# Hybrid decoder trunk on one core: head sums taken token by token, SSD decays taken from banks that exist, and a conformer tail in token halves

## The chip, the cores and the metric

The kernel runs on 1 core of one Trainium2 chip. Times are device microseconds of one execution; a time is the median of several runs. Engines are named as the profile names them: PE (TensorE), PEld (its weight loads), DVE (VectorE), ACT (ScalarE), POOL (GpSimd) and SP (SyncE, which issues the transfers). The profiler took one execution; its page and its trace tell where that execution's time lies.

## The reference, cut to what matters

```python
D_MODEL, SEQ = 1024, 512
# layer 0: combined projection -> SSD heads and sliding-window attention -> output projection, residual
cb       = einsum("bclgn,bcsgn->bgcls", cc, bc)
y_diag   = einsum("bgecls,bcsgep->bclgep", cb[:, :, None] * decay_in, x)
y_off    = einsum("bclgn,bcgepn,bgecl->bclgep", cc, states, exp(a_cs))   # a_cs: running sum per head
y        = y_diag + y_off + xf * d_skip
y        = gated_group_rms_norm(y, z, w, groups)                        # two groups, y * silu(z)
q, k     = rms_norm(q, q_norm_w), rms_norm(k, k_norm_w)                  # per head of 64 channels
...      # windowed softmax with a sink per head and a T5 relative bias
# layer 1: conformer module
a, gate  = split(rms_norm(x) @ pw1 + pb1)
u        = a * sigmoid(gate)
v        = causal_depthwise_conv(u, dw, dwb)                             # 31 taps, 1024 channels
v        = silu(layer_norm(v, lnw, lnb))                                 # mean and variance over 1024 channels
x        = x + v @ pw2 + pb2
# behind each layer: gated MLP (D_FF = 2816) with a causal convolution of width 3, residual
```

## The kernel before, in words

512 tokens lie in the free dimension, 1024 channels in 8 tiles of 128 partitions. The program is the mixer (SSD and attention), a feed-forward block, the conformer, a second feed-forward block. Each large product takes float32 inputs split into a high and a low part, so each 128 x 128 block of weights costs three matmuls of 512 columns (L135 to L137); weights come three tiles ahead through `wr`, ACT casts the high part (L119) and DVE subtracts the low one (L120). A PSUM tile is called a bank: "mm" for products, "pa", "pb", "pc" for the rest.

In the mixer a scheduler orders the instructions of each engine; dependences, the number of buffers of a tag and the order of the code decide. A loop goes over x and q tiles: a projection, and beside it the SSD work of one head pair j. `ssd_states` spreads the row of each head over 128 partitions with a matmul (L483) for the mask exponentials. `ssd_outputs` multiplies masks and inputs (L515), spreads the pair's rows a second time with `pair_bcast` (L269), takes the exponential (L519) and multiplies it (L523) with the carried states' product (L522). `head_sums` squares a q or k tile (L535), casts and subtracts it into two parts (L537, L539) and adds, with two matmuls (L542), the sums over the two heads of 64 channels into rows of one bank `st_q`. After the last tile those rows are copied by ACT (L585) and transposed to token-wise columns (L588), and the inverse square roots of all heads are taken at once (from L593). Behind the attention `gr`, the inverse square root of the gated norm's moments, is spread over partitions (L163) before the output projection can go on.

The conformer is written out by hand: every engine runs its instructions as the code stands, within `manual_schedule`. Weight tiles are loaded in the order of use by SP. `project(2j)` gives the value, `project(2j+1)` the gate of tile j. `gate(j)` scales the gate (L863), takes the sigmoid (L865), forms `u` (L867), writes it to memory (L871) and reads it back in four shifted copies (L873) into `u4`, a tag of three buffers. `conv_pe(j)` convolves four taps at a time from these copies (L884, 24 groups of 4; 32 groups for tile 7) and subtracts a shift (L890); `add` and `sums` fold the result into running sums. `conv_pe(7)` runs in token halves. `tail_sums` (L941), `moments`, `spread` (L958), `normalise`, `residue` and `outputs` (L983 to L985) finish each half.

Of the kernel before, what the change touches and what calls it, by code (L numbers as in the profile page):

```python
# [7 lines left out]
F32 = mybir.dt.float32  # L8
F32R = mybir.dt.float32r
# [49 lines left out]
def kernel(ctx: ExitStack, tc: tile.TileContext, x, w_in, w_dt, w_out,  # L59
# [164 lines left out]
    def mixer(norm, nxt):  # L224
# [26 lines left out]
        sels = [mk([P, P], f"sel{i}", F32R) for i in range(2)]  # L251
        turn = [0]

# [4 lines left out]
        def pair_bcast(tag, j, r0):  # L258
            sel = sels[turn[0] % 2]
            if j == 8:  # L260
                for t in sels:
                    clear(t[64:P])
            turn[0] += 1
            a, b = (j, j + 8) if j < 8 else (16, 17)
            rr = slice(r0, r0 + 64)
            for half, q in zip(HALF, (a, b)):
                V.tensor_copy(sel[rr, half], con("pairs")[rr, q : q + 1].to_broadcast([64, 64]))
# [155 lines left out]
        for t in sels:  # L423
            clear(t[0:64])
        halves = mk([P, 265], "halves", F32R)
        V.tensor_copy(halves, con("halves"))
# [43 lines left out]
        def ssd_states(j):  # L470
# [21 lines left out]
            ssd[j] = [xdt, ms, xdd]  # L492
# [16 lines left out]
        def ssd_outputs(j):  # L509
            g = j // 4  # L510
            xdt, ms, sm = ssd.pop(j)
# [101 lines left out]
        bank = pair_bcast("pa", 8, 0)  # L613
# [14 lines left out]
        def attn_prep(j):  # L628
            bt = phase[0].tile([P, 2, 256], F32, name=nm("bt"), tag="bt", bufs=2)
            nc.sync.dma_start(bt, btab[j])  # L630
            bank = pair_bcast("pa", j, 0)
# [174 lines left out]
    def conformer(norm, nxt):  # L806
# [25 lines left out]
        def load(i):  # L832
            raws[i] = sbt("wr", 3, RING)
            nc.sync.dma_start(raws[i], pw1[(i % 2) * 8 + i // 2] if i < 16 else pw2[i - 16])
# [26 lines left out]
        def gate(j, va, pg):  # L861
            vg = sbt("cv", 2)
            V.tensor_tensor(vg, pg, norm.rb, op=ALU.mult)  # L863
            sg = sbt("th", 1)
            S.activation(sg, vg, AF.Sigmoid, bias=prm("pb1", 8 + j))  # L865
            u = ubuf[j % 3]
# [8 lines left out]
        def conv_pe(j, q=None, part=None):  # L875
            n, t0 = (T, 0) if q is None else (H, H * q)
            npe = GROUPS_PE[j]
            if part in (None, 0):
                cvp[j, q] = bank_of("pa")
            cv = cvp[j, q]  # L880
            gs = range(npe) if part is None else range(npe // 2 * part, npe // 2 * (part + 1))
            for g in gs:
# [323 lines left out]
```

## Time and profile before

| | |
|---|---|
| median of 3 runs | 1295.35 us |
| range of the runs | 1294.02 to 1297.88 us |
| profiled execution | 1297.84 us, its span 1296.0 us |
| mean granted TensorE clock | 0.996 |
| busy share of the span | PE 99%, DVE 66%, ACT 40%, POOL 10% |
| norm sums that open the first feed-forward block, the conformer, the second feed-forward block | at 381.7, 742.6 and 936.9 us |

The page gives busy time per engine and the chain that ended last. A busy PE includes matmuls that run at half clock, and the end of a matmul is modelled, so gaps on PE are read from the starts in the timeline and from the releaser in brackets. The windows view gives the granted clock of a stretch.

### The profile page before, as it was taken

Reading aid. Unit: us, or ns where it says so; the run is one execution under the profiler, and the core shown is the slowest. Engines: PE = TensorE matmul, PEld = TensorE weight load, DVE = VectorE, ACT = ScalarE, POOL = GpSimd, SP = SyncE. Lnnn points to the kernel's source line nnn. Section 1 sums busy time; section 2 is a strip of 40 time slices with the busy share of each in tenths; the row PEclk is TensorE's granted clock in tenths of the full one; section 3 lists DMA queues with packets and bytes.
Section 4 is the critical chain, followed back from the end, with each engine's and each line's share of the span. In section 5 each row is a group of like instructions: output and inputs, shape, how many; then the busy total and the mean of one; then the engine's idle time right before and its main releaser. Section 6 shows DMA issues by size and latency. Waiting matters only on the chain.

```text
span 1296.0 us, 16832 instructions
## 1 busy us (share of the span) xinstructions
PE 1281.3 (99%) x6443; PEld 1032.4 (80%) x6443; DVE 854.4 (66%) x1444; ACT 515.2 (40%) x812; POOL 124.2 (10%) x198
## 2 busy tenths in 40 slices
PE   9999999999999999999999999999999999999998
PEld 7878877778888888888888876658888888888887
DVE  7986769985348777777332377857677777774221
ACT  6465547863234333333232222226433333332120
POOL 0031204640210000000011100000600000000000
PEclk9999999999999999999999999999999999999999
DMA  6312222212333333323333265550333333333331
GB/s 225 98 50 65 66 65 66 66 44 71 98 101 96 96 95 96 96 94 94 102 90 103 90 181 146 154 151 2 117 98 98 98 98 98 96 92 102 108 118 39
DMA packets 40113, 125.13 MB, mean 97 GB/s; under 512 B 4704, under 2 KB 5088, under 8 KB 40032
## 3 DMA queue, kind: packets, MB, share of 16 engines
q1 hardware_dynamic: 39312, 123.50, 31.2%
q8 instruction: 51, 0.84, 0.3%
q10 hardware_dynamic: 720, 0.55, 0.2%
q14 instruction: 30, 0.25, 0.1%
HBM read 119.73 MB, written 4.29 MB: 96 GB/s over the span
## 4 chain that ended last, share of the span: by engine, by line
PE 78%; DVE 2%; POOL 0%; DMA 0%; issue 0%; ACT 0%; SPq 0%; ACTq 0%; POOLq 0%
PE mm L135 23%; PE mm L137 23%; PE mm L136 23%; PE pa L884 3%; PE pc L690 1%; PE pa L136 1%; PE pa L137 1%; PE pa L135 1%; PE pb L681 1%; DMA u<-du 0%; PE pb L163 0%; PE mm L984 0%; PE mm L985 0%; PE mm L983 0%; POOL lt L665 0%
## 5 line engine op out<-in xcount | busy, mean ns | idle before, releaser
L135 PE MATMUL mm<-xr,wh 128*128 128x512 f32 x1120 | 439.1, 392 | 0.0
L137 PE MATMUL mm<-xr,wl 128*128 128x512 f32 x1120 | 437.2, 390 | 0.5 <-DVE wl L362 0.5
L136 PE MATMUL mm<-xr,wh 128*128 128x512 f32 x1120 | 437.2, 390 | 0.0
L119 ACT CAST wh<-wr 128x1024 fp32r<-128x1024 f32 (+1 forms) x178 | 184.0, 1034 | 453.6 <-PE mm L136 411.3
L120 DVE TENSOR_TENSOR wl<-wr,wh 128x1024 fp32r<-128x1024 f32 (+1 forms) x178 | 214.5, 1205 | 156.2 <-ACT wh L119 151.0
L137 PEld LDWEIGHTS mm<-xr,wl 128*128 128x128 f32 x1120 | 210.3, 188 | 44.6 <-DVE wl L362 1.0
L135 PEld LDWEIGHTS mm<-xr,wh 128*128 128x128 f32 x1120 | 210.4, 188 | 43.6 <-issue 1.4
L136 PEld LDWEIGHTS mm<-xr,wh 128*128 128x128 f32 x1120 | 210.4, 188 | 43.0 <-DVE xr L183 0.4
L221 DVE TENSOR_TENSOR cv<-mm,nrb 128x512 f32<-128x512 f32 x116 | 79.6, 689 | 94.4 <-PE mm L137 90.4
L136 PE MATMUL mm<-g,wh 128*128 128x512 f32 x360 | 140.0, 389 | 0.0
L135 PE MATMUL mm<-g,wh 128*128 128x512 f32 x352 | 136.9, 389 | 0.0
L137 PE MATMUL mm<-g,wl 128*128 128x512 f32 x352 | 136.9, 389 | 0.0
L216 DVE SCALAR_TENSOR_TENSOR ct<-cv,par_ffn,ct 128x510 f32<-128x510 f32 (+1 forms) x176 | 131.1, 748 | 3.5 <-issue 0.4
L136 PEld LDWEIGHTS mm<-g,wh 128*128 128x128 f32 x360 | 67.6, 188 | 14.1
L135 PEld LDWEIGHTS mm<-g,wh 128*128 128x128 f32 x352 | 66.1, 188 | 13.7
L137 PEld LDWEIGHTS mm<-g,wl 128*128 128x128 f32 x352 | 66.1, 188 | 13.6
L193 POOL TENSOR_TENSOR nsum<-nsum,nsq 128x512 f32<-128x512 f32 x21 | 34.3, 1631 | 427.0 <-ACT nsq L192 427.0
L213 ACT ACTIVATE ct<-cv,par_ffn 128x512 f32<-128x512 f32 x88 | 71.4, 814 | 3.2 <-DVE cv L221 3.0
L789 ACT ACTIVATE th<-ct 128x512 f32<-128x512 f32 x44 | 27.8, 632 | 84.5 <-DVE ct L216 84.5
L800 DVE TENSOR_TENSOR h<-h,mm 128x512 f32<-128x512 f32 x16 | 11.0, 687 | 56.3 <-PE mm L137 56.3
L884 PE MATMUL pa<-u,dg 128*32 128x512 f32 (+1 forms) x464 | 45.0, 535 | 1.4 <-DMA u<-du 1.4
L884 PEld LDWEIGHTS pa<-u,dg 128*32 128x32 f32 x464 | 14.5, 110 | 27.0 <-issue 21.5
(308 smaller groups left out, 1393.4 us busy)
## 6 DMA issues: line engine op xcount, KB each, us to landing
wr<-w_up SPq DMA_DIRECT2D x88, 512.0 KB, 3.5
wr<-w_in SPq DMA_DIRECT2D x29, 512.0 KB, 3.5
wr<-w_dn SPq DMA_DIRECT2D x32, 448.0 KB, 3.3
wr<-pw SPq DMA_DIRECT2D x24, 512.0 KB, 6.0
wr<-w_out SPq DMA_DIRECT2D x16, 512.0 KB, 3.6
wr<-w_dn SPq DMA_DIRECT2D x16, 512.0 KB, 3.5
u<-du SPq DMA_DIRECT2D x28, 266.0 KB, 5.0
h<-x SPq DMA_DIRECT2D x8, 256.0 KB, 5.6
```

The source lines that it names most:

```text
L119: S.copy(wh[:, :n], raw[:, :n])
L120: V.tensor_tensor(wl[:, :n], raw[:, :n], f32(wh[:, :n]), op=ALU.subtract)
L135: TE.matmul(bank, wh[:, c], xh, start=first and i == 0, stop=False)
L136: TE.matmul(bank, wh[:, c], xl, start=False, stop=False)
L137: end = TE.matmul(bank, wl[:, c], xh, start=False, stop=last and i == n - 1)
L193: eng.tensor_tensor(self.sum, self.sum, sq, op=ALU.add)
L213: S.activation(t, v, AF.Identity, bias=bias, scale=w(taps - 1))
L216: V.scalar_tensor_tensor(t[:, s:], v[:, : T - s], w(k), t[:, s:], op0=ALU.mult, op1=ALU.add)
L221: V.tensor_tensor(v, bank, rb, op=ALU.mult)
L681: TE.transpose(tb[:, blk(b * 2 + e)], lt[:, e, blk(b)], ident)
L789: S.activation(sg, c, AF.Silu)
L884: TE.matmul(cv[quad(c), :n], diag[j][:, g, c, :], u4[j][:, c, 4 * g + t0 : 4 * g + t0 + n], start=g == 0, stop=g == npe - 1 and j < 2)
```

## The change

Three places change.

**SSD decays.** `ssd_states` takes, from the two banks it has anyway, an exponential of half the partitions each into `ec`, kept in the tag "att" until `ssd_outputs`. The second spread with `pair_bcast`, its two DVE casts and its exponential go. `pair_bcast` now serves the q and k scaling alone.

**Head sums.** The square, unsplit, is the stationary operand: four matmuls, each 128 tokens by 2 columns, write the sums token by token into `st_q`. The cast, the subtraction, the two matmuls of 512 columns, the copy and the four transposes go.

**Conformer.** The gate is projected first and its sigmoid taken before the value's projection ends; the loads swap accordingly. `gate(7)` is issued before the last part of `taps(6)`. The convolution of tile 4 moves out of the loop behind the sixteenth projection. Tiles 5 and 6 are convolved in token halves, interleaved with tile 7, whose first half now comes before the second halves of 5 and 6. The shifted copies of tile 7 are read in two parts (284 and 256 of 540 columns). The first output step comes before the second half's sums; the second evacuation on ACT stands behind the second `normalise`.

```diff
-        def pair_bcast(tag, j, r0):
+        def pair_bcast(tag, j):
...
@@ ssd_states
             ms = []
+            ec = sbt("att", 16)
             for e in range(2):
                 hd = e * 8 + j
                 bank = bank_of("pa")
                 TE.matmul(bank, pairs[:, hd : hd + 1].to_broadcast([P, P]), rows_t, start=True, stop=True)
+                S.activation(ec[HALF[e], P:], bank[HALF[e], P:], AF.Exp)
...
@@ ssd_outputs
-            cb2 = pair_bcast("pa", j, 64)
-            ec = sbt("d", 3)
-            S.activation(ec[:, P:], cb2[:, P:], AF.Exp)
...
@@ head_sums
-            hi = sbt("cv", 2, T, F32R)
-            V.tensor_copy(hi, sq)
-            lo = sbt("th", 1, T, F32R)
-            V.tensor_tensor(lo, sq, f32(hi), op=ALU.subtract)
-            w = halves[:, 137:265] if n == 8 else halves[:, 9 - n : 137 - n]
-            for i, o in enumerate((hi, lo)):
-                TE.matmul(st_q, w, o, start=n == 8 and i == 0, stop=n == 7 and i == 1)
+            for c in range(NB):
+                cols = slice(c * 18 + n, c * 18 + n + 9, 8) if n < 8 else slice(c * 18 + 16, c * 18 + 18)
+                TE.matmul(st_q[:, cols], sq[:, blk(c)], halves[:, 9:18:8], start=True, stop=True)
...
-        ssum = sbt("d", 3)[0:32]
-        S.copy(ssum, st_q[0:32])
-        bank = bank_of("pb")
-        for c in range(NB):
-            TE.transpose(bank[:, c * 32 : (c + 1) * 32], ssum[:, blk(c)], ident[0:32, 0:32])
-        stv = bank[:, : NB * 32].rearrange("p (c k) -> p c k", c=NB)[:, :, 0:18]
+        stv = st_q[:, : NB * 18].rearrange("p (c k) -> p c k", c=NB)
...
@@ conformer: gate
-            for s in range(4):
-                nc.sync.dma_start(u4[j][quad(s), :, 0:n], du.rearrange("(c p) n -> p c n", c=4)[:, :, s : s + n])
+            first = H + 4 * (GROUPS_PE[j] - 1)
+            for a, b in ((0, first), (first, n)) if j == 7 else ((0, n),):
+                for s in range(4):
+                    nc.sync.dma_start(u4[j][quad(s), :, a:b],
+                                      du.rearrange("(c p) n -> p c n", c=4)[:, :, s + a : s + b])
...
@@ conformer: order
-                if j >= 2:
+                if 2 <= j < 6:
                     conv_pe(j - 2)
...
-            conv_pe(5)
-            add(5)
-            sums(5)
-            conv_pe(6)
-            add(6)
-            sums(6)
-            conv_pe(7, 0, 0)
-            conv_pe(7, 0, 1)
+            gate(7, pa, sg)
+            taps(6, 1)
+            conv_pe(4)
+            add(4)
+            sums(4)
+            conv_pe(5, 0)
+            conv_pe(6, 0)
+            conv_pe(7, 0)
             evacuate(0)
-            conv_pe(7, 1, 0)
+            conv_pe(5, 1)
             bank = tail_sums(0)
             lr = moments(bank)
-            conv_pe(7, 1, 1)
-            evacuate(1)
+            conv_pe(6, 1)
             sa = spread(lr)
-            bank = tail_sums(1)
+            conv_pe(7, 1)
...
```

What stood on PE in one iteration of the mixer's loop before (`cv` and `th` are the two parts of the square, `b` the masks, `rows_t` the rows of decays, `bc` the states; the rows run from the head sums to the next pair's spread):

```order
L542 MATMUL mm_515<-cv_1084,halves 128x512
L515 MATMUL pb_1090<-b_985,c_973 64x128
...
L515 MATMUL pb_1090<-b_995,c_973 64x128
L542 MATMUL mm_515<-th_1086,halves 128x512
L515 MATMUL pb_1090<-b_985,c_973 64x128
...
L269 MATMUL pa_1101<-rows_t,sel_86 128x512
L522 MATMUL pc_1105<-bc_440,d_1043 128x128 x3
L474 MATMUL pb_1112<-ctile,xs_997 128x128 x4
```

And what stands there now, with the lines of the changed program (L531 is the head sums, L511 the mask products, L515 the states' product):

```order
L531 MATMUL mm_513<-ctile,nsq_1072 128x2 x4
L511 MATMUL pb_1078<-b_974,c_960 64x128
L511 MATMUL pb_1078<-b_985,c_960 64x128
...
L515 MATMUL pc_1087<-bc_438,d_1033 128x128 x3
L468 MATMUL pb_1094<-ctile,xs_987 128x128 x4
```

Three matmuls of 512 columns became four of 2 columns, and the eight mask products are no longer parted in two. Nine tiles have such sums; eight pairs had such a spread.

DVE at the gated norm before, from the last gate product to the last operation on `gr` (`nvar` is the moment, `rsi`, `rsh`, `rsq` steps of the inverse square root):

```order
L120 TENSOR_TENSOR wl_3356<-wr_3353,wh_3355 128x1024
L718 SCALAR_TENSOR_TENSOR ct_3174<-th_3172,cv_3170 128x512
L733 TENSOR_SCALAR nvar_3185<-pb_3180 128x4
L719 TENSOR_TENSOR xs_1429<-xs_1429,ct_3174 128x512
L142 TENSOR_SCALAR rsi_3188<-nvar_3185 128x4
...
L736 TENSOR_SCALAR gr_3187<-gr_3187 128x4
```

And in the changed program:

```order
L717 TENSOR_SCALAR nvar_3130<-pb_3125 128x4
L120 TENSOR_TENSOR wl_3301<-wr_3298,wh_3300 128x1024
L702 SCALAR_TENSOR_TENSOR ct_3119<-th_3117,cv_3115 128x512
L142 TENSOR_SCALAR rsi_3133<-nvar_3130 128x4
L146 TENSOR_SCALAR rsh_3136<-nvar_3130 128x4
L703 TENSOR_TENSOR xs_1404<-xs_1404,ct_3119 128x512
...
L720 TENSOR_SCALAR gr_3132<-gr_3132 128x4
```

The moment now stands ahead of the weight subtraction and of the last gate product. On PE 33 matmuls of the gate's projection stand between the attention's last product and the sums, where 12 stood, and 23 of the output projection between the sums and the spread of `gr`, where 25 stood.

PE in the conformer's tail before (`u` are the shifted copies, `dg` the taps on a diagonal, `krows,neg` the shift):

```order
L884 MATMUL pa_7335<-u_1408_7125,dg_7046 32x512 x24
L890 MATMUL pa_7335<-krows,neg 128x512
L884 MATMUL pa_7372<-u_1425_7242,dg_7163 32x512 x24
L890 MATMUL pa_7372<-krows,neg 128x512
L884 MATMUL pa_7409<-u_1440_7328,dg_7274 32x256 x32
L890 MATMUL pa_7409<-krows,neg 128x256
L884 MATMUL pa_7447<-u_1440_7328,dg_7274 32x256 x16
...
L884 MATMUL pa_7447<-u_1440_7328,dg_7274 32x256 x16
L890 MATMUL pa_7447<-krows,neg 128x256
L958 MATMUL pb_7520<-ctile,lr_7478 128x128 x4
```

And now (L873 is the convolution, L879 the shift, L932 the sums, L949 the spread):

```order
L873 MATMUL pa_7253<-u_1363_6953,dg_6864 32x512 x24
...
L873 MATMUL pa_7290<-u_1380_7070,dg_6991 32x256 x24
...
L873 MATMUL pa_7327<-u_1395_7156,dg_7108 32x256 x24
...
L873 MATMUL mm_7358<-u_1410_7239,dg_7188 32x256 x32
...
L873 MATMUL pa_7290<-u_1380_7070,dg_6991 32x256 x24
...
L932 MATMUL pb_7428<-ones,s_1259_6357 128x1
...
L873 MATMUL pa_7327<-u_1395_7156,dg_7108 32x256 x24
...
L949 MATMUL pb_7493<-ctile,lr_7442 128x128 x4
L873 MATMUL mm_7358<-u_1410_7239,dg_7188 32x256 x32
```

The whole convolution of tile 4 and half of those of tiles 5 and 6 now stand ahead of the first half of tile 7; behind the first half's sums stand a half of tile 6, the spread and the second half of tile 7.

## Rows read from the trace of the kernel before

**Rows 1.** The page's parts 1 and 4: busy time of each engine with its share of the span, and the chain of work that ended last, by engine.

```profile
PE 1281.3 (99%) x6443; PEld 1032.4 (80%) x6443; DVE 854.4 (66%) x1444; ACT 515.2 (40%) x812; POOL 124.2 (10%) x198
...
PE 78%; DVE 2%; POOL 0%; DMA 0%; issue 0%; ACT 0%; SPq 0%; ACTq 0%; POOLq 0%
```

**Rows 2.** The windows view, four stretches of the span. Columns: stretch, its length; busy time of PE, PEld, DVE, ACT and POOL (instructions); granted TensorE clock; DMA share; GB/s.

```profile
88.00:176.00 88.00, 88.00 (x488) 71.17 (x487) 59.75 (x112) 45.61 (x95) 19.00 (x24) 1.00 0.23 72
200.00:276.00 76.00, 73.42 (x561) 56.85 (x561) 68.61 (x232) 60.21 (x176) 44.91 (x123) 1.00 0.18 57
...
288.80:295.40 6.60, 6.60 (x23) 5.73 (x23) 5.42 (x11) 3.06 (x5) 0.00 (x0) 0.50 0.26 79
...
882.80:886.00 3.20, 3.15 (x13) 2.98 (x14) 2.89 (x14) 2.07 (x4) 0.00 (x0) 0.50 0.00 0
```

**Rows 3.** The timeline of PE in the loop over x and q tiles, in one iteration (91.32 to 94.61) and in the last one (169.56, 170.58). Columns: start, duration, engine, line, operation, count [idle before <- releaser].

```profile
91.32 0.39 PE L542 MATMUL mm<-cv,halves 128*128 128x512 f32 x1
...
92.23 0.50 PE L542 MATMUL mm<-th,halves 128*128 128x512 f32 x1
...
93.24 0.51 PE L269 MATMUL pa<-rows_t,sel 128*128 128x512 f32 x1
93.58 0.83 PE L522 MATMUL pc<-bc,d 128*128 128x128 f32 x6
94.25 0.60 PE L474 MATMUL pb<-ctile,xs 128*128 128x128 f32 x4
...
169.56 1.09 PE L515 MATMUL pb<-b,c 128*64 128x128 f32 x16
170.58 0.50 PE L269 MATMUL pa<-rows_t,sel 128*128 128x512 f32 x1
```

**Rows 4.** The timeline of PE at another place of the kernel that takes sums over the 128 channels of a tile with a matmul of one column (`tok_sum`, four matmuls, eight records), between two projections of the feed-forward block.

```profile
381.68 0.95 PE L157 MATMUL pb<-ones,nsum 128*128 128x1 f32 x8
382.49 0.48 PE L135 MATMUL mm<-xr,wh 128*128 128x512 f32 x1
382.81 0.40 PE L136 MATMUL mm<-xr,wh 128*128 128x512 f32 x1
383.04 0.39 PE L137 MATMUL mm<-xr,wl 128*128 128x512 f32 x1
```

**Rows 5.** The lines view of ACT between 60 and 300 us, shapes apart: count | busy, mean ns of one | idle before.

```profile
L519 ACT ACTIVATE d<-pa 128x384 f32<-128x384 f32 x8 | 3.9, 491 | 2.1 <-PE pa L269 2.1
```

**Rows 6.** The timeline of all engines at the end of the head sums, from the square of the last q tile to the transposes.

```profile
178.59 0.63 ACT L535 ACTIVATE nsq<-att 128x512 f32<-128x512 f32 x1
...
179.79 0.69 DVE L539 TENSOR_TENSOR th<-nsq,cv 128x512 fp32r<-128x512 f32 x1
...
180.54 0.19 PEld L542 LDWEIGHTS mm<-th,halves 128*128 128x128 f32 x1 [0.26 <-DVE th L539]
...
181.88 0.32 PEld L588 LDWEIGHTS pb<-ctile,d 32*128 32x128 f32 x4 [0.35 <-ACT d L585]
```

**Rows 7.** The timeline of DVE at the gated norm of the mixer: one step of the inverse square root, and the last operation on `gr`.

```profile
285.70 1.20 DVE L149 TENSOR_TENSOR rsq<-rsy 128x4 f32<-128x4 f32 x1
...
287.91 0.17 DVE L736 TENSOR_SCALAR gr<-gr 128x4 f32<-128x4 f32 x1
```

**Rows 8.** The timeline of PE at the same place: the last matmul ahead of the broadcast of `gr`, the broadcast itself, and the output projection behind it.

```profile
285.81 0.39 PE L135 MATMUL mm<-att,wh 128*128 128x512 f32 x1
288.23 1.53 PE L163 MATMUL pb<-ctile,gr 128*128 128x128 f32 x8 [2.03 <-DVE gr L736]
289.56 1.71 PE L157 MATMUL pb<-ones,bc 128*128 128x1 f32 x8
291.12 0.77 PE L136 MATMUL mm<-att,wh 128*128 128x512 f32 x1
...
295.54 0.44 PE L137 MATMUL mm<-att,wl 128*128 128x512 f32 x1
```

**Rows 9.** The timeline of PE in the tail of the conformer, from the end of the sixteenth projection (runs of equal matmuls in one row).

```profile
856.16 5.36 PE L884 MATMUL pa<-u,dg 128*32 128x512 f32 x48
...
861.88 5.36 PE L884 MATMUL pa<-u,dg 128*32 128x512 f32 x48
...
869.07 3.66 PE L884 MATMUL pa<-u,dg 128*32 128x256 f32 x64 [1.40 <-DMA u<-du]
...
872.98 1.93 PE L884 MATMUL pa<-u,dg 128*32 128x256 f32 x32
874.84 0.38 PE L941 MATMUL pb<-ones,s 128*128 128x1 f32 x2
...
876.72 1.93 PE L884 MATMUL pa<-u,dg 128*32 128x256 f32 x32
...
879.60 1.16 PE L958 MATMUL pb<-ctile,lr 128*128 128x128 f32 x8 [0.63 <-DVE lr L152]
...
882.85 0.58 PE L983 MATMUL mm<-dg,wh 128*128 128x256 f32 x1 [0.41 <-ACT dg L973]
...
888.37 0.39 PE L984 MATMUL mm<-g,wh 128*128 128x256 f32 x1 [0.70 <-DVE g L976]
```

**Rows 10.** The timeline of DVE and SP in the same stretch: the gated `u` of tile 7, and the issue of its four shifted copies.

```profile
858.19 0.75 DVE L867 SCALAR_TENSOR_TENSOR u<-cv,par_conf,th 128x512 f32<-128x512 f32 x1 [0.85 <-ACT th L865]
...
861.57 1.75 SPq L873 DMA_DIRECT2D u<-du  x4
```

More of the change, by code (lines that the diff above doesn't have):

```diff
@@ L256, in clear @@
             V.tensor_copy(t, f32(t))
-        def pair_bcast(tag, j, r0):
+        sels = [mk([P, P], f"sel{i}", F32R) for i in range(2)]
+        turn = [0]
+        def pair_bcast(tag, j):
             sel = sels[turn[0] % 2]
-            if j == 8:
-                for t in sels:
-                    clear(t[64:P])
             turn[0] += 1
[L264 to L267, printed above, removed]
+            for half, q in zip(HALF, (j, j + 8) if j < 8 else (16, 17)):
+                V.tensor_copy(sel[0:64, half], con("pairs")[0:64, q : q + 1].to_broadcast([64, 64]))
             bank = bank_of(tag)
@@ L859, in make_diag, with sigmoid, gate @@
             diag[j] = t
-        def gate(j, va, pg):
-            vg = sbt("cv", 2)
-            V.tensor_tensor(vg, pg, norm.rb, op=ALU.mult)
+        def sigmoid(j, pg):
+            vg = scaled(pg, norm.rb)
             sg = sbt("th", 1)
             S.activation(sg, vg, AF.Sigmoid, bias=prm("pb1", 8 + j))
+            return sg
+        def gate(j, pa, sg):
+            va = scaled(pa, norm.rb)
             u = ubuf[j % 3]
@@ L888, in conv_pe @@
                 TE.matmul(cvp["shift"], neg, krows, start=True, stop=True)
-            if j > 1 and part in (None, 1):
-                TE.matmul(cv[:, :n], neg, krows[:, t0 : t0 + n], start=False, stop=True)
+            if j > 1:
+                TE.matmul(cv, neg, krows[:, t0 : t0 + n], start=False, stop=True)
         def taps(j, part):
@@ L901, in taps, with add, sums @@
                     V.scalar_tensor_tensor(y[j], win(j, k), w(j, k), y[j], op0=ALU.mult, op1=ALU.add)
-        def add(j):
-            V.tensor_tensor(y[j], cvp.pop((j, None)), y[j], op=ALU.add)
-        def sums(j):
+        def add(j, q=None):
+            t = slice(0, T) if q is None else half(q)
+            V.tensor_tensor(y[j][:, t], cvp[j][:, t], y[j][:, t], op=ALU.add)
+        def sums(j, q=None):
+            t = slice(0, T) if q is None else half(q)
             if j == 0:
@@ L1000, in conformer @@
                 if j > 0:
-                    va = scaled(pa, norm.rb)
-                if j >= 2:
+                    sg = sigmoid(j, pg)
+                if 2 <= j < 6:
                     conv_pe(j - 2)
@@ L1005, in conformer @@
                     shift_mean()
-                pg = project(2 * j + 1)
+                pa = project(2 * j + 1)
                 if j == 0:
                     norm.spread()
-                    va = scaled(pa, norm.rb)
+                    sg = sigmoid(j, pg)
                 split_w(2 * j + 3)
@@ L1020, in conformer @@
                         sums(q)
-                if j >= 4:
+                if 4 <= j < 6:
                     sums(j - 2)
-                gate(j, va, pg)
-            pa = project(14)
+                gate(j, pa, sg)
+            pg = project(14)
             make_diag(7)
             split_w(16)
+            sg = sigmoid(7, pg)
             taps(6, 0)
-            va = scaled(pa, norm.rb)
-            pg = project(15)
+            pa = project(15)
             split_w(17)
+            gate(7, pa, sg)
@@ L1051, in conformer @@
+            add(6, 1)
+            sums(6, 1)
             sa = spread(lr)
-            bank = tail_sums(1)
-            obank = [bank_of(t) for t in ("mm", "mm", "mm", "pc")]
-            normalise(0, 0, sa)
-            for j in range(1, 8):
+            conv_pe(7, 1)
+            obank = [bank_of(t) for t in ("mm", "mm", "pc", "mm")]
+            for j in range(5):
+                normalise(j, 0, sa)
+                if j:
+                    residue(j - 1, 0)
+                if j == 1:
+                    evacuate(1)
@@ L1056, in conformer @@
+            outputs(0, 0)
+            lr = moments(tail_sums(1))
+            for j in range(5, 8):
                 normalise(j, 0, sa)
                 residue(j - 1, 0)
-                if j == 2:
-                    lr = moments(bank)
             residue(7, 0)
-            for j in range(8):
+            for j in range(1, 8):
                 outputs(j, 0)
-                if j == 4:
+                if j == 5:
                     sa = spread(lr)
```

57 lines of the change are left out of this document (29 added, 28 removed).

## The prediction, made before the changed kernel had run

> **What bounds the kernel now.** I read the page's busy times and chain first, then the windows of the stages that change, then PE's timeline in them. PE is busy 99% of the span and the chain of waits lies on PE for 78% [rows 1]: what the change takes out of PE's queue shows in the time, what it takes from other engines does not. The windows add that PE is not one thing everywhere. In the loop over x and q tiles PE is busy 88.00 of 88 us, DVE 59.75 and ACT 45.61; in the attention PE is busy 73.42 and DVE 68.61 of 76, so DVE sets part of the pace there; and two short stretches, 6.60 and 3.20 us, ran at the 0.50 granted clock, the lower of the two levels (1.2 for 2.4 GHz) [rows 2]. The two gaps worth having are at those two stretches: 2.03 us ahead of the spread of `gr` [rows 8] and some waits in the conformer's tail [rows 9].
>
> **Head sums and second spread, on PE.** In one iteration the stretch from the first 512-column sum (91.32) to the next pair's transposes (94.25) takes 2.93 us [rows 3]. What is left of it: sixteen mask products without a break, 169.56 to 170.58, 1.02; the states' product, 93.58 to 94.25, 0.67 [rows 3]. What comes in: four matmuls of two columns. The nearest row is the sum of one column over 128 channels, 128 weights each, eight records, 381.68 to 382.49, 0.81 [rows 4]. So 1.02 + 0.67 + 0.81 = 2.50, a gain of 0.43 each. Five iterations have both edits: -2.15. Two further spreads stand without sums: 93.24 to 93.58, 0.34 each [rows 3], -0.68. The last iteration has sums and spread with 0.23 + 0.33 + 0.34 against 0.81: -0.1. Three sums stand alone amid projections, where the old pair costs about 0.47 (two at the 0.23 spacing seen at 382.81 to 383.04) and the new 0.81 plus 0.09 by which the second matmul behind it is late (382.49 to 382.81 against 0.23) [rows 4]: +0.43 each, +1.3, a little less where the old pair stood apart. The four transposes go: about -0.4 [rows 6]. Sum -2.1. The bounds are what eight small records can cost: nothing beyond their issue would add another -6 (nine groups by 0.7); 1.2 each would eat it (+3.5). I keep the row.
>
> A page of the Trainium skill has a rule here: "TensorE: Matmul & The Clock Gate", section "Back-to-back issue gap", puts matmuls of 1 to 64 columns at an issue floor of about 25 ns. By it eight records would cost 0.2 us instead of 0.8, an estimate from that figure, and nine groups would give 5.4 us more. The row disagrees: 0.10 us for each record, each with 128 columns of weights to load.
>
> **The chain behind the head sums.** The last square ends at 179.22; the casts, the subtraction, the second matmul at 180.54, ACT's copy and the transposes at 181.88 follow [rows 6]. All but the sums go, so k and q scaling can begin some 1.4 us sooner. PE has projections to do meanwhile, so this moves work but does not add to the sum.
>
> **The exponentials.** ACT gives up eight of 491 ns [rows 5] and takes sixteen of the same width over half the partitions. I price them alike: +3.9 us over eight pairs, 0.5 each. ACT is busy 45.61 of 88 us there [rows 2], which hides them. They hold a "pa" bank 0.5 us longer ahead of the mask exponentials; if that cover is gone, the price is 8 x 0.5 = 4 at most.
>
> **The gated norm.** PE stands 2.03 us for `gr` [rows 8]. In the changed order the moment's first operation stands ahead of a weight subtraction and of the last gate product on DVE, and PE has two matmuls less (0.5 us) between sums and spread. Counted in DVE operations, `gr` then comes about as PE does, with 0.2 us to spare. Yet one step of four columns on DVE took 1.20 us where the last operation on `gr` took 0.17 [rows 7], a hold-up on DVE that may stay. I take 1.4 of the 2.03 as gained; ends 0 and 2.03.
>
> **The slow clock behind it.** After that gap PE ran 6.6 us at 0.50, until a matmul at 295.54 [rows 2, 8]; at full clock the same work takes half, 3.3. The wait of 1.40 at 869.07 was followed by no such row in the windows I read [rows 9], so a wait cut to about 0.6 should not bring the clock down. -3.3, and 0 as the other end.
>
> **The conformer's tail.** PE's work from the end of the sixteenth projection (856.16) is the same list as before plus the convolution of tile 4, which only changes place (5.72, as 856.16 to 861.88 [rows 9]). Splitting tiles 5 and 6 adds two more shifts of 256 columns and four more starts, about +0.8. What can go: waits of 1.40 (shifted copies), 0.63 (`lr`), 0.41 (`normalise`) and 0.70 (`residue`) [rows 9], together 3.14, and the 3.20 us at 0.50 [rows 2] which cost 1.5. Each is covered now: between first sums and their spread stands a half convolution of tile 6 (half of 5.72) against a chain of 2.9 (876.72 to 879.60 [rows 9]); between spread and outputs stands the second half of tile 7, 3.9 (869.07 to 872.98 [rows 9]); the first output step and the sums of the second half, 1.9 (874.84 to 876.72), give `normalise` time. -3.14 - 1.5 + 0.8 = -3.8.
>
> Against it stand the copies of tile 7. `u4` has three buffers, so they now wait for tile 4's convolution, which ends 5.3 us after 856.16 [rows 9]: 861.5. Before, they were issued at 861.57, after a round through memory that follows `u`, done at 858.94 [rows 10]; the sigmoid's early place saves nothing there, since the wait has taken its place. From issue to use it took 7.5 us before (861.57 to 869.07 [rows 9, 10]). PE reaches tile 7 now after 5.72 and two halves of about 3.07, 868.0. If the first part lands in the share of its bytes (284 of 540: 3.9 us) nothing waits; if each part costs as the whole, 1.1 us are lost; interleaved with the weights, up to 2.7. I take 0.3. Tail: -3.5.
>
> [...]
>
> **Sum.** -2.1 - 1.4 - 3.3 - 3.5 = -10.3. The profiled execution took 1297.84, which is 2.5 above the median, so I apply the difference to the median: 1295.35 - 10.3 = 1285.05.
>
> **The rivals.**
> (a) The stall at `gr` stays or moves, and the clock falls as before. Its support is the DVE step of 1.20 us [rows 7]. Left are -2.1 and -3.5: 1289.7.
> (b) The mixer's saving is lost in the attention, where DVE is busy 68.61 of 76 us [rows 2]: PE arrives sooner and waits longer, the stall stays, and the copies come 1 to 2 us late. Only some -2 to -3 is left: 1292.8. For it: DVE's share. Against: PE has projections to put between.
> (c) Slower. Each group of eight small records is 0.8 us in which PE moves few columns, and if the granted clock fell behind each of nine groups as it did behind `gr`, each would cost 3.3 [rows 2]: +30, less the 10 gained, about 1315. It decides from about four such falls. Against it: behind the group at 381.68 matmuls run at 0.23 spacing at once [rows 4].
> (d) The edits do their work, but PE's queue is short of ready projections throughout, and nothing changes: 1295.
>
> **How the numbers follow.** Forecast 0.48, (a) 0.32, (b) 0.12, (c) 0.05, (d) 0.03. 0.3% of 1295.35 is 3.9 us, about what a measurement of this kernel can tell from no change. Faster than 1291.5: the forecast, (a) and nearly half of (b), 0.85. Within: 0.10. Slower: 0.05. The forecast's own ends: -12.4 with the whole stall and a tail of -5, and another 2.5 if the attention's own gaps of 2.58 us [rows 2] shrink: 1280.5. Upward the range takes in (a) and the better half of (b): 1291.5. Left out is less than 0.2.
>
> **What would show it.** One iteration of the mixer at 2.5 us from the sums to the next transposes; eight records of the head sums at 0.8 us; no wait over 1 us ahead of the spread of `gr` and no 0.50 behind it; tile 7's first half starting behind tile 6's without a gap; the first output step without a wait, at clock 1.00. The prediction fails if the small matmuls bring the clock down, if a bank held for the new exponentials stops PE in the loop, or if the copies come late.

## The result, and the profile after

The changed kernel takes 1288.77 us (median of 5 runs, 1288.48 to 1288.92); before, on the same chip, took 1295.35 (5 runs, 1293.77 to 1297.88). The ratio is 0.9943, with a 95% interval of 0.9932 to 0.9955: faster by 6.6 us, where 10.3 were forecast. Its profiled execution took 1288.92, with a span of 1287.1 and a mean clock of 1.000; that of before had 1297.84, 1296.0 and 0.996, so the two profiles differ by 8.9.

The page's parts 1 and 4 of the changed kernel answer [rows 1]:

```profile
PE 1274.5 (99%) x6583; PEld 1035.6 (80%) x6583; DVE 839.2 (65%) x1411; ACT 518.8 (40%) x821; POOL 124.0 (10%) x198
...
PE 78%; DVE 2%; POOL 1%; DMA 1%; issue 0%; ACT 0%; SPq 0%; DVEq 0%; ACTq 0%; POOLq 0%
```

PE is busy 6.8 us less with 140 records more; the share of the chain is as before. So the page tells that time went from PE, not where. One iteration of the loop in PE's timeline answers [rows 3]:

```profile
90.32 0.95 PE L531 MATMUL mm<-ctile,nsq 128*128 128x2 f32 x8
91.20 1.09 PE L511 MATMUL pb<-b,c 128*64 128x128 f32 x16
92.22 0.94 PE L515 MATMUL pc<-bc,d 128*128 128x128 f32 x6
93.00 0.60 PE L468 MATMUL pb<-ctile,xs 128*128 128x128 f32 x4
```

From the sums to the transposes 93.00 - 90.32 = 2.68 us instead of 2.93; 2.50 was forecast. Eight small records take 0.88 here, where 0.81 was priced, and the states' product 0.78 for 0.67.

PE's timeline at the gated norm answers [rows 8], with the windows view of the stretch behind it (columns as in [rows 2]):

```profile
285.03 0.39 PE L136 MATMUL mm<-att,wh 128*128 128x512 f32 x1
286.20 1.13 PE L163 MATMUL pb<-ctile,gr 128*128 128x128 f32 x8 [0.78 <-DVE gr L720]
287.17 0.95 PE L157 MATMUL pb<-ones,bc 128*128 128x1 f32 x8
287.98 0.48 PE L137 MATMUL mm<-att,wl 128*128 128x512 f32 x1
288.29 0.39 PE L135 MATMUL mm<-att,wh 128*128 128x512 f32 x1
```

```profile
284.00:290.00 6.00, 5.22 (x32) 4.33 (x31) 3.49 (x9) 1.63 (x2) 1.04 (x1) 1.00 0.05 18
```

The wait of 2.03 us is 0.78, and the clock behind it is 1.00. The conformer's tail answers [rows 9]:

```profile
846.31 5.36 PE L873 MATMUL pa<-u,dg 128*32 128x512 f32 x48
851.60 0.50 PE L879 MATMUL pa<-krows,neg 128*128 128x512 f32 x1
852.03 2.80 PE L873 MATMUL pa<-u,dg 128*32 128x256 f32 x48
...
855.07 2.80 PE L873 MATMUL pa<-u,dg 128*32 128x256 f32 x48
...
858.18 3.66 PE L873 MATMUL mm<-u,dg 128*32 128x256 f32 x64
...
862.09 2.80 PE L873 MATMUL pa<-u,dg 128*32 128x256 f32 x48
...
869.76 1.10 PE L949 MATMUL pb<-ctile,lr 128*128 128x128 f32 x8
870.78 3.66 PE L873 MATMUL mm<-u,dg 128*32 128x256 f32 x64
874.38 0.39 PE L879 MATMUL mm<-krows,neg 128*128 128x256 f32 x1
874.60 0.28 PE L974 MATMUL mm<-dg,wh 128*128 128x256 f32 x1
```

No row carries a wait in brackets: not the first half of tile 7 (858.18), not the spread (869.76), not the first output step (874.60). The waits of 1.40, 0.63, 0.41 and 0.70 are gone together.

The waits view of PE, over the whole span (columns: who waits for whom; us in total, times, longest us), names what is left:

```profile
PE pb L665 <- POOL lt L649: 2.4, 3, 1.0
PE pb L163 <- DVE gr L720: 1.1, 2, 0.8
...
PE pa L873 <- DMA u<-du: 0.4, 1, 0.4
```

The first row is in the attention, where before had less. The last is new. The same row of before:

```profile
PE pb L681 <- POOL lt L665: 1.0, 2, 0.5
```

**Where the time went, by stage.** The next table is worked out from the starts of PE's matmuls in each profiled execution: A from the first norm's sums to the gated norm's, B to the norm sums of the first feed-forward block, C from the conformer's norm sums to the sums over tile 0, D from there to the second feed-forward block's norm sums. In before D ends at 936.70. The first feed-forward block (360.9) and the end, up to PE's last matmul (355.3), are equal in all. The programs below the second row are the experiments. The last column says in which stages, and for how many us, the granted clock of the profiled execution was 0.50. By the difference in B between before and e1, 6.8 us cost 3.2; 3.4 us cost about half of that, an estimate.

| program | A | B | C | D | us at clock 0.50 |
|---|---|---|---|---|---|
| before | 256.79 | 102.26 | 45.45 | 148.69 | B 6.8, D 3.4 |
| changed | 256.89 | 97.97 | 45.94 | 143.79 | none |
| before again (e1) | 256.77 | 99.03 | 45.45 | 148.81 | D 6.8 |
| decays alone (e12) | 255.09 | 102.27 | 45.46 | 149.93 | B 6.8, D 6.8 |
| head sums alone (e4) | 259.20 | 97.89 | 45.45 | 152.71 | D 3.4 and 6.8 |
| mixer alone (e2) | 256.93 | 97.91 | 45.45 | 150.07 | D 3.4 |
| conformer alone (e3) | 256.79 | 98.98 | 46.41 | 143.72 | none |
| changed again (e5) | 256.86 | 97.98 | 45.87 | 143.73 | none |
| copies in one part (e6) | 256.93 | 97.89 | 45.49 | 147.82 | D 3.4 |
| tile 4 back in the loop (e7) | 256.98 | 97.89 | 46.01 | 150.36 | D 3.4 |
| attention copies on ACT (e8) | 257.00 | 97.78 | 46.59 | 143.73 | none |
| additions on DVE (e9) | 257.31 | 96.70 | 45.70 | 143.73 | A 3.4 |
| first gate early (e10) | 256.97 | 97.91 | 45.45 | 144.10 | none |
| both (e11) | 257.33 | 96.69 | 45.45 | 144.19 | A 3.4 |

Between the two profiles B gives 4.3 us and D 4.9, C takes 0.5, and A, in which the mixer's edits lie, gives nothing. The rest is 0.4 us of the start. Where the table shows a stage of the same code at different times (D of before, e1, e2, e4 and e12), the differences are falls of the clock and waits, and one execution of each was profiled.

### The profile page after: what moved, and what is told of

It is laid out like the page before. It is cut to its first block, busy times and chain, and to the rows that moved or that the text cites. A ratio compares the mean times of both kernels' runs of the same rounds, so it can differ in the third digit from the quotient of the medians.

```text
span 1287.1 us, 17080 instructions
## 1 busy us (share of the span) xinstructions
PE 1274.5 (99%) x6583; PEld 1035.6 (80%) x6583; DVE 839.2 (65%) x1411; ACT 518.8 (40%) x821; POOL 124.0 (10%) x198
## 4 chain that ended last, share of the span: by engine, by line
PE 78%; DVE 2%; POOL 1%; DMA 1%; issue 0%; ACT 0%; SPq 0%; DVEq 0%; ACTq 0%; POOLq 0%
PE mm L135 23%; PE mm L137 23%; PE mm L136 23%; PE pa L873 3%; POOL lt L649 1%; PE pa L135 1%; PE pa L137 1%; PE pa L136 1%; PE mm L873 1%; PE pc L674 1%; PE pb L665 1%; PE mm L974 0%; DMA u<-du 0%; PE mm L975 0%; PE mm L976 0%; PE pb L163 0%
## 5 line engine op out<-in xcount | busy, mean ns | idle before, releaser
L221 DVE TENSOR_TENSOR cv<-mm,nrb 128x512 f32<-128x512 f32 x124 | 85.1, 689 | 95.0 <-PE mm L137 91.0
L873 PE MATMUL pa<-u,dg 128*32 128x512 f32 (+1 forms) x432 | 38.0, 499 | 0.4 <-DMA u<-du 0.4
L649 POOL TENSOR_SCALAR lt<-lt,rec 128x256 f32<-128x256 f32 (+1 forms) x64 | 33.1, 531 | 38.4 <-DVE rec L647 38.2
```

Source lines behind the costliest of these rows:

```text
L221: V.tensor_tensor(v, bank, rb, op=ALU.mult)
L649: G.tensor_scalar(lt[:, e, s0:256], lt[:, e, s0:256], rec[:, e : e + 1], 0.0, op0=ALU.mult, op1=ALU.add)
L873: TE.matmul(cv[quad(c)], diag[j][:, g, c, :], u4[j][:, c, 4 * g + t0 : 4 * g + t0 + n], start=g == 0, stop=g == npe - 1 and j < 2)
```

## The experiments

Theory 1 says that a part of the gain is the clock, which falls in some executions of before only. Theory 2 says that the attention, at DVE's pace, takes what the mixer's edits save on PE.

**e1, the kernel before once more.**

> The kernel before, once more, to see what its executions differ in. Theory 1 (the clock): the profiled execution of before holds stretches at half clock behind the spread of gr and in the tail (3.3 and about 1.8 us by its trace), and other executions lack one or both; then times above 1296 carry a mean clock of 0.997 or less, times below 1294.5 one of 0.999 or more, and the spread of the times is 3 to 5 us. Rival: all executions have the same clock, and the times differ by waits; then the clock is the same to 0.001 over the whole range.

Measured: 1297.46 us (11 runs), ratio 1.0004 (0.9994 to 1.0013). Times and mean clocks of its runs, in order: 1293.90 at 0.998, 1294.08 at 0.999, 1295.18 and 1296.97 at 0.997 and 0.996, five from 1297.16 to 1297.66 at 0.996, 1298.10 and 1298.36 at 0.994. Theory 1 holds in the main. Over all 72 executions of before on record with a clock (these and those measured beside the experiments) the median time is 1294.6 us at a mean clock of 0.999, 1295.8 at 0.997, 1297.4 at 0.996 and 1298.1 at 0.994. But the ranges overlap: times of 1294.13 at 0.997 and 1296.38 at 0.999 miss the signs named beforehand, as 1293.90 at 0.998 does, so the clock is not all that differs. The profiled execution of e1 had the same wait for `gr` as before, and no fall behind it; PE's timeline and the windows view:

```profile
288.69 1.13 PE L163 MATMUL pb<-ctile,gr 128*128 128x128 f32 x8 [2.03 <-DVE gr L736]
289.66 0.95 PE L157 MATMUL pb<-ones,bc 128*128 128x1 f32 x8
```

```profile
290.00:296.00 6.00, 6.00 (x30) 5.06 (x30) 5.52 (x13) 3.15 (x6) 0.00 (x0) 1.00 0.26 87
```

So stage B with the wait alone is 99.03, with the fall 102.26: the fall costs 3.2, as priced, and comes in some executions. The fall of e1 lies in the tail, twice as long as that of before [rows 2], and begins 2 us behind a wait of 0.64 us, amid sums of one column:

```profile
879.00:885.70 6.70, 6.70 (x32) 6.57 (x32) 5.77 (x26) 3.49 (x7) 0.00 (x0) 0.50 0.00 0
```

**e2, the mixer's edits alone** (the hunks of the diff up to the attention, none of the conformer's).

```diff
+            for c in range(NB):
+                TE.matmul(st_q[:, cols], sq[:, blk(c)], halves[:, 9:18:8], start=True, stop=True)
...
+                S.activation(ec[HALF[e], P:], bank[HALF[e], P:], AF.Exp)
```

> The two mixer edits alone (decays and head sums), the conformer as before. Theory 2 (the attention takes the saving): PE saves 2.1 us ahead of the attention and waits as much more in it, so what is left is the shorter wait for gr and its clock, 2 to 4 us: 1291.5 to 1293.5, and the sums ahead of gr start within 0.5 us of before's 279.4. Rival (PE bound throughout): the 2.1 us show as well, the sums start 2 us earlier, and the time is 1289 to 1291.

Measured: 1296.20 (11 runs) beside 1296.40, ratio 0.9998 (0.9988 to 1.0009): no gain, where 2 to 4 us were expected. Stage A is as before and B 1.1 below e1, as theory 2 said. In the profiled execution (1294.31 us) the miss is in D, whose code is that of before: 150.07, 1.3 more than e1. PE's timeline of it and the windows view behind that row show why:

```profile
883.36 0.58 PE L968 MATMUL mm<-g,wh 128*128 128x256 f32 x1 [1.93 <-DVE g L960]
```

```profile
883.40:886.60 3.20, 3.20 (x15) 3.20 (x16) 2.93 (x8) 2.95 (x6) 0.00 (x0) 0.50 0.02 5
```

Before has that wait with 0.70 [rows 9], behind outputs at half clock. Here the outputs ahead of it ran at clock 1.00 (877.8 to 883.3), so PE came sooner to the same late operand, and the clock fell behind the wait, for 3.4 us as in before. In before's tail the fall covered a part of the wait; here both are paid in full. What the other ten executions lost in D was not profiled.

**e3, the conformer's edits alone** (the other hunks).

```diff
-            for j in range(7):
-                pa = project(2 * j)
+                pg = project(2 * j)
...
+            conv_pe(5, 0)
+            conv_pe(6, 0)
+            conv_pe(7, 0)
```

> The conformer edits alone, the mixer as before. Theory 1 and the trace of the changed kernel: the tail gives 4.9 us in an execution where before ran its tail at half clock for 3 us and 3.1 in one where it did not, and the first tile's copies cost 0.5: 1290.5 to 1292.5. The wait of 2 us for gr and its half clock stay, so the times still spread by 2 us or more. Rival: the tail was hidden in part by work at the second half's end; then 1293 or more.

Measured: 1293.56 (7 runs, 1289.76 to 1294.18), ratio 0.9969 (0.9958 to 0.9981). The median is 1.1 above the expected range and within the rival's, but the rival's reason does not hold: D is 143.72, 5.1 below e1, so the tail gave all that was expected. C is 1.0 above, with a wait of 0.93 for the first copies. The runs at clock 1.000, of which the profiled one showed no fall, take 1289.76 and 1290.77, those at 0.997 about 1293.6 to 1294.2. That these fall behind `gr`, where the wait is still 2.02 us, fits their distance and is inferred; none of them was profiled.

**e4, the head sums alone**, and **e12, the decays alone**.

> The token-wise head sums alone. Theory 2: eight small records (0.8 us) stand for two wide matmuls (0.7 with the break they make), so PE's work is the same within 0.5 us, the chain behind the sums is 1.4 us shorter, and the attention takes that: 1293.5 to 1296. Rival A: the shorter chain shows, 1293 or less. Rival B: the small matmuls cost more than the row says, slower than 1297.

> The decay edit alone: before with the second spread taken out, head sums as before. By the sums over PE's starts, eight spreads of 0.35 us go and the two spreads that stay cost 0.7 more: -2.0 on PE ahead of the attention. Theory 3 (waits depend on where POOL's additions fall in the attention, not on the pace of DVE): the order there may stay as before, and the 2 us show, the stretch from the first to the gated norm's sums falls from 256.8 to about 254.8. Rival (the attention takes any saving): it stays at 256.8.

Measured: e4 1299.12 (11 runs) beside 1296.40, ratio 1.0019 (1.0010 to 1.0028), slower than expected. e12 1297.25 (11 runs) beside 1296.18, ratio 1.0005 (0.9997 to 1.0014). In e12, A falls by 1.70: a saving on PE ahead of the attention does show in A, and theory 2's "takes any saving" is wrong. It does not show in the median: in the profiled execution D is 149.93, 1.1 above e1, since PE waits 2.55 us for the copies of tile 7 (1.44 in e1), and B has the fall. In e4, A rises by 2.41. The sums over PE's starts in A, by function, tell what did it:

| us on PE in A | before | decays alone | head sums alone | changed |
|---|---|---|---|---|
| projections (672 matmuls) | 162.24 | 162.07 | 161.32 | 161.11 |
| `pair_bcast` | 5.05 | 2.35 | 4.98 | 2.28 |
| `head_sums` | 5.86 | 5.84 | 7.69 | 7.68 |
| transposes of the sums | 0.36 | 0.36 | 0 | 0 |
| `ssd_states`, `_carry`, `_outputs` | 27.72 | 29.00 | 27.04 | 27.88 |
| attention, logits and values | 48.18 | 48.16 | 50.77 | 50.64 |
| attention stage, first logits to last values | 75.37 | 75.34 | 77.02 | 76.82 |
| of it, projections (their number) | 25.57 (93) | 25.55 (93) | 24.70 (94) | 24.67 (94) |
| of it, PE's waits over 0.15 us | 1.22 | 1.23 | 2.39 | 2.39 |

The attention's matmuls, the same 464 in each, cost 2.5 us more wherever the token-wise sums are in, and nothing more where only the decays are. The projections that the scheduler puts between them cost 0.9 less there, so that the attention stage as a whole is 1.65 us longer in e4 and 1.45 in the changed kernel; 1.2 of it are waits of PE that before does not have. Outside this stage A is 1.7 us shorter than before in e12, 0.8 longer in e4 and 1.35 shorter in the changed kernel: the saving on PE is that of the decays, and the head sums cost PE time by themselves. What they gave is the shorter wait for `gr`: B is 97.89 in e4 and 102.27, with wait and fall, in e12. Rival B of e4 has the time right and not the reason, since a small record costs what the row said (7.69 / 72 = 0.107 us). PE's waits in the two, by the waits view, head sums alone first:

```profile
PE pa L874 <- DMA u<-du: 3.5, 1, 3.5
PE pb L671 <- POOL lt L655: 2.4, 3, 1.0
```

```profile
PE pb L163 <- DVE gr L730: 2.0, 1, 2.0
...
PE pb L675 <- POOL lt L659: 1.0, 2, 0.5
```

The first row of e4 is a second cost, in the tail, whose code it shares with before: PE waited 2.0 us longer than in e1 for the copies of tile 7, and 1 us behind that wait the clock fell to 0.50 for 3.4 us. Their way through memory took 4.4 us there and 2.4 in e1, by the transfers view from 856 to 861 us (columns: KB each, us to landing; a queue's packets, MB and share of the engines' time):

```profile
q8 instruction: 1, 0.02, 2.2%
issues: line engine op xcount, KB each, median us to landing
du<-u SPq DMA_DIRECT2D x1, 271.5 KB, 4.4
```

In e4 one packet of instruction code lay in the same 5 us; 2.2% of 16 engines is 1.8 us of one. In e1 there was none. That this packet held one engine's share back is an inference from the two traces; it wasn't isolated.

**e5, the changed kernel again.**

> The changed kernel again, on the chip of this call, beside the kernel before. Theory 1 (the clock): both places at which before's clock falls are gone, so all times lie within 0.7 us at a mean clock of 0.999 or more, 1288 to 1289.5, while before spreads over 4 us. Rival: the small spread on the first chip was chance; then some times lie 2 us higher at a clock under 0.998.

Measured: 1288.49 (5 runs, 1288.37 to 1288.97, clocks 0.999 and 1.000) beside 1296.56 (17 runs, 1293.87 to 1298.72), ratio 0.9934 (0.9922 to 0.9945). Of those 17 runs of before the six at 0.999 take 1293.87 to 1295.58, the eleven at 0.996 and 0.994 take 1296.08 to 1298.72. The changed kernel's gain is 5.4 to 7.1 us against the first and 7.6 to 10.2 against the second.

**e6, the copies in one part**, and **e7, tile 4's convolution back in the loop**.

```diff
-            for a, b in ((0, first), (first, n)) if j == 7 else ((0, n),):
+            for a, b in ((0, n),):
```

> The changed kernel with tile 7's shifted copies read in one part again, four transfers of 540 columns. By the trace of the changed kernel the copies are issued 5.9 us after the sixteenth projection and PE wants the first half at 11.8; whole copies took 7.5 us from first issue to use, so 1.3 to 1.7 us of waiting come back: 1290 to 1290.6. Rival (the two halves share the same engines and give nothing): 1288.3 to 1289.2.

```diff
-                if 2 <= j < 6:
+                if j >= 2:
                     conv_pe(j - 2)
...
-            conv_pe(4)
             split_w(18)
-            add(4)
-            sums(4)
```

> The changed kernel with the convolution of tile 4 back in the loop, ahead of the thirteenth pair's second projection. PE's work is the same; it reaches tile 7's first half 5.7 us sooner after the sixteenth projection, at 6.1 us, while the copies cannot land before about 9 to 10. Theory (holding back covers the copies): a wait of 3 to 4.5 us, 1291.5 to 1293.5, and more where the clock falls behind it. Rival: the copies start sooner, since their buffer is free, and land in time; within 1 us of the changed kernel.

Measured: e6 1292.54 (6 runs), e7 1295.40 (11 runs), beside e5's 1288.49 on the same chip: 4.1 and 6.9 us, both above the expected ranges, though e7's allowed for more where the clock falls. PE's timeline at tile 7's first half, with the windows view behind it, e6 and then e7:

```profile
859.96 5.35 PE L873 MATMUL mm<-u,dg 128*32 128x256 f32 x64 [2.33 <-DMA u<-du]
```

```profile
860.50:863.80 3.30, 3.30 (x39) 2.01 (x33) 0.00 (x0) 0.00 (x0) 0.00 (x0) 0.50 0.03 12
```

```profile
863.22 5.20 PE L873 MATMUL mm<-u,dg 128*32 128x256 f32 x64 [4.96 <-DMA u<-du]
```

```profile
863.20:866.30 3.10, 3.08 (x32) 1.73 (x36) 0.00 (x0) 0.00 (x0) 0.00 (x0) 0.50 1.07 285
```

The waits are 2.33 and 4.96, somewhat over what was expected (1.3 to 1.7, and 3 to 4.5), and the 64 matmuls behind them take 5.35 and 5.20 instead of 3.66, since the clock is 0.50 in more than half of that time. In these executions halving the transfer and holding work back each pay twice: the wait, and the clock behind it. Not every run of e6 loses as much: its fastest, 1289.41, is within 1 us of the changed kernel. In the changed kernel the first part lands in 2.9 us (median of four issues), in e6 the whole in 4.9. The Trainium skill ("DMA: Bandwidth & Descriptors", section "Rules for kernel authors") speaks against two transfers to halves of the partitions, since they share the engines. Here the parts lie along the tokens, the user takes them one after the other, and the run decides for them.

**e8, copies of the attention on ACT**, and **e9, additions on DVE.** After e2 and before e12, these tried what paces the attention: DVE's sum of work, or (theory 3) additions of 1.3 us in POOL's queue ahead of its products.

```diff
-            if c % 2:
+            if c % 2 or c == 0:
                 S.copy(pt[:, o0:], tb[:, o0:])
```

> The changed kernel with the eight copies of 256 columns in the attention (0.42 us each) on ACT instead of DVE. Theory 2 (the attention runs at DVE's pace and took the mixer's 2.1 us): DVE loses 3.3 us of work there, and 1 to 2.5 us come out: 1286.3 to 1287.8, the sums ahead of gr starting sooner by as much. Rival: the pace is set by the chain of one head (logits, maximum, exponential, reciprocal, POOL's product), not by DVE's sum of work; then within 0.5 us of the changed kernel or slower.

```diff
-                G.tensor_tensor(gs[g], gs[g], sq, op=ALU.add)
+                V.tensor_tensor(gs[g], gs[g], sq, op=ALU.add)
```

> The changed kernel with the six additions of the gated norm's squares (1.3 us each) on DVE instead of POOL. Theory 3 (POOL's queue took the mixer's saving: an addition of 1.3 us stands ahead of the attention's products, and PE waits for those products): PE's waits for POOL's product in the attention, 2.4 us in the changed kernel and 1.0 in before, fall to 1 or less, and 1 to 2.5 us come out, 1286 to 1287.5. Rival (DVE is the pace there, busy 86 of 96 us): another 4 us on DVE make it slower, 1289.5 or more.

Measured: e8 1289.07 (5 runs, 1287.95 to 1289.70), no gain over 1288.49; e9 1287.55 (5 runs, 1286.66 to 1288.12). In e8 the attention ends 6 us sooner, yet A stays at 257.00: fewer projections lie within it (67 for 94), and its logits and values still cost 50.50. Theory 2 falls by this too; 0.65 of e8's time is a longer wait for the first copies in C. In e9 POOL's wait falls from 2.4 to 1.2, but a wait of 0.68 for ACT comes, logits and values cost 51.48, and A is no shorter. What e9 gains, about 1 us, it gains in B (96.70): PE does not wait for `gr` at all, its timeline says

```profile
286.41 1.05 PE L163 MATMUL pb<-ctile,gr 128*128 128x128 f32 x8
```

Yet e9 does not speak against theory 3. Behind the two waits, which end at 260.67 and 262.63, the windows view has a fall of the clock in the attention that no other program but e11 shows:

```profile
262.70:266.10 3.40, 3.40 (x20) 2.61 (x22) 2.15 (x8) 2.98 (x11) 2.22 (x6) 0.50 0.13 49
```

It costs about 1.7 us, half of 3.4. Without it A would be about 255.6 and not 257.31, an estimate, and that is 1.2 less than before: about what the mixer's edits save on PE outside the attention. So additions in POOL's queue may be most of what the attention took back. That is not shown, since no execution of e9 or e11 without the fall was profiled. POOL's timeline of the changed kernel shows one of them in the making, with PE's row behind it:

```profile
206.41 1.31 POOL L710 TENSOR_TENSOR bc<-bc,nsq 128x512 f32<-128x512 f32 x1
207.68 0.76 POOL L640 COPY lt<-nsink 128x1 f32<-128x1 f32 x2
208.42 1.37 POOL L649 TENSOR_SCALAR lt<-lt,rec 128x256 f32<-128x256 f32 x2
...
209.39 1.00 PE L665 MATMUL pb<-ctile,lt 128*128 128x128 f32 x4 [0.82 <-POOL lt L649]
```

**e10, the first tile's gate early, and e11, e9 and e10 together.** In C the changed kernel waits 0.42 us for the first copies. Its timeline of ACT and DVE there:

```profile
746.09 1.28 ACT L848 ACT_TABLE_LOAD   x1
...
747.38 0.72 ACT L848 ACTIVATE th<-cv,par_conf 128x512 f32<-128x512 f32 x1
748.01 1.98 ACT L828 CAST wh<-wr 128x1024 fp32r<-128x1024 f32 x2
749.08 1.23 DVE L829 TENSOR_TENSOR wl<-wr,wh 128x1024 fp32r<-128x1024 f32 x1 [2.29 <-ACT wh L828]
750.22 0.68 DVE L221 TENSOR_TENSOR cv<-mm,nrb 128x512 f32<-128x512 f32 x1
```

With the sigmoid first, ACT loads its table ahead of the weight cast, DVE's subtraction waits for that cast, and the value's scaling stands behind the subtraction.

```diff
+                    sig = phase[0].tile([P, 1], F32, name="sig")
+                    S.activation(sig, ones[:, 0:1], AF.Sigmoid)
                     norm.spread()
                     sg = sigmoid(j, pg)
+                    gate(j, pa, sg)
                 split_w(2 * j + 3)
```

> The changed kernel with the first tile's gate ahead of the weight split behind it, and the sigmoid's table loaded before the norm is there. Theory: PE's wait of 0.42 us for the first tile's shifted copies, which the kernel before did not have, goes, and the stretch from the conformer's norm sums to the next sums falls from 45.9 to 45.5 us: 1288.0 to 1288.3. Rival: the copies' landing varies by itself, and nothing changes.

> Both of the two edits before. If they are independent, their gains add up: 1285.5 to 1287.2 under theory 3; if theory 3 falls, the time of the additions on DVE less 0.4.

Measured: e10 1288.44 (5 runs), e11 1287.55 (5 runs), no more than without the edit. C falls to 45.45 as expected, in e11 too, and the first copies are issued 3.9 us sooner behind the norm sums (after 12.95 us for 16.86). But the rival has a point: the wait differs from run to run without the edit (0.42, 0.39, none in e6, 0.53 in e7, 1.08 in e8), and e6's C is 45.49. D rises by 0.3 (144.10): 0.6 us more in the projections, which I did not follow up. e9 and e11 are the fastest kernels that were run, 0.9929 (0.9915 to 0.9942) and 0.9930 of before.

## Why the prediction was right or wrong

The direction and the range held: 1288.77 lies within 1280.5 to 1291.5, near rival (a) (1289.7), not at 1285.0. That it is near (a) is chance: in (a) the stall at `gr` stays or moves and the clock falls as before, and neither happened. Between the two profiles 8.9 us were gained, of 10.3 forecast, and that too is in part luck: the mixer gave 2.2 us less on PE than its step said and the first tile took 0.5, while the tail gave 1.4 more. By its steps:

- **Head sums and second spread on PE, -2.1.** Too much, and the destination was wrong. Outside the attention stage A fell by 1.35: by function -2.7 for the spreads, +1.8 for the sums, -0.4 for the transposes and -0.1 for the rest. One iteration gives 0.25 where 0.43 was forecast. Then the attention stage took 1.45, and A ended where it was. The step that failed is the sentence that PE "has projections to do meanwhile, so this moves work but does not add to the sum". Rival (b) said that the attention would eat the saving, at DVE's pace; e8 and e12 show that the pace of DVE is not why. The loss comes with the head sums edit (e4, e12), with another order of PE and POOL in the attention. Of the 1.45, 1.2 are waits of PE, those for POOL above all; that POOL's additions cause them is likely by e9 and not shown, and the rest is open.
- **Eight small records, 0.81.** They cost 7.68 us over nine groups, 0.85 a group and 0.107 a record. The row was the right price. The Trainium skill ("TensorE: Matmul & The Clock Gate", section "Back-to-back issue gap") gives an issue floor of about 25 ns for so few columns, and says of its formula that it is an isolated gap which at small N leaves weight loads out. In this case 128 columns of weights are loaded for each record, and its trace does not come near the floor. With 7.68 for 5.86 the head sums by themselves are dearer on PE than before, and the breaks that they spare elsewhere do not make this even: in e4 A outside the attention is 0.8 longer.
- **Exponentials, nothing.** Held for ACT: they take 0.47 to 0.49 us each, and no row of PE in the loop waits for them. But with the decays came one wait of 0.56 us for a mask of POOL's, at 79.82 (0.57 in e12, none in before and e4); POOL makes that mask behind an addition that waits for `ec`'s product. No step had it.
- **The gated norm, -1.4.** Measured -1.25 at the first spread (2.03 to 0.78), less 0.3 that is now waited at the second: B is 1.06 below e1.
- **The slow clock behind it, -3.3.** The size was right, 3.2 by B of before and e1. The step that failed is "I apply the difference to the median": the fall is in the profiled execution of before, but only in a part of its runs. So the sum on the median was too large by about the 2.5 us that lay between the profile of before and its median. That those 2.5 us are this fall is inferred from the times and clocks in e1; of the five runs of before only one was profiled.
- **The conformer's tail, -3.5.** Measured -4.9 between the two profiles, all of it in D. The copies cost nothing where 0.3 was kept. By sums over PE's starts in D, the half clock and the waits ahead of the outputs gave 3.1 (outputs 25.76 to 23.32, token sums 4.13 to 3.48) instead of 2.6, and the convolutions, with 2.0 of waits in them, fell by 1.7 (38.69 to 36.99): the halves added 0.3 instead of 0.8. That the copies wait for tile 4's convolution follows from the three buffers of `u4` and was harmless: their way through memory ended at 852.20, after it (851.60).
- **Missed altogether:** the first tile's wait, +0.5 in C, since no step looked at the order of ACT's queue at j = 0.
- **Rival (c)** did not occur: the clock is 1.00 throughout the loop.

## What to carry to other kernels

Before a gain read in one profile is put on the median, see whether the stretch at half clock stands in other executions too: run the kernel before once more, and set times against clocks. Removing a wait pays most where the clock falls behind it, and two edits that each remove one of two such places were worth 0.2 and 2.8 us of the median alone (e2, e3) and 8.1 together (e5): with one place left, 7 of 11 and 5 of 7 runs still had a mean clock of 0.998 or less. So set stages against each other, and not only medians, when an edit is tried alone. A saving ahead of a stage that a scheduler has interleaved is counted only where that stage's order stays as it was.

## What was not expected of the hardware

The same program with the same wait of 2.03 us went on at clock 1.00 in one execution (e1) and at 0.50 for 6.8 us in another (before). In the tail the clock fell to 0.50 for 3.4 us at the end of waits of 2.33 (e6), 3.47 (e4) and 4.96 us (e7), give or take 1 us, but not behind one of 2.55 us (e12); behind 0.78 us and less at `gr` none of the profiled ones slowed. Yet a short wait is no safeguard: in e1's tail the clock fell, for 6.8 us, behind a single wait of 0.64 us and sums of one column. The same sums stand in the tail of the changed kernel, without a wait, and no profiled execution without a wait in its tail fell there. The write of 271.5 KB to memory took 2.4 (e1) to 4.4 us (e4) in programs whose code there is the same.
